# Cosine-similarity attention on one core: joint sums of squares as sixteen matmuls into one block of 64 columns, and new engine orders

## The chip, the core and the metric

The kernel runs on one core of one Trainium2 chip. The metric is the device time of one execution in microseconds (us). The profile shows one execution: PE is TensorE (matmuls), PEld its weight loads, DVE is VectorE, ACT is ScalarE, POOL is GpSimd, SP is the engine that issues most DMAs.

## What is computed

```python
Q_norm = Q / (np.linalg.norm(Q, axis=-1, keepdims=True) + 1e-10)
K_norm = K / (np.linalg.norm(K, axis=-1, keepdims=True) + 1e-10)
scores = np.einsum('bhqd,bhkd->bhqk', Q_norm, K_norm) / tau      # tau = 0.1
weights = np.exp(scores - np.max(scores, axis=-1, keepdims=True))
weights = weights / (np.sum(weights, axis=-1, keepdims=True) + 1e-10)
return np.einsum('bhqk,bhkd->bhqd', weights, V).astype(np.float32)
```

Q, K and V are float32 with 8 batches, 12 heads, 512 rows and 64 columns.

## The kernel before

The 96 heads are worked on in 48 pairs. Each pair s goes through the same steps, and the steps have keys that the order lists and this text use:

- LD and LV load Q, K and V of the pair (SP issues, 256 KB each) into rings of 15 and 10 buffers. VC casts V to bf16 beside a column of ones (POOL, L657).
- SQ squares Q and K of the pair into one bf16 tile `sq` of 16 groups (8 of Q, then 8 of K) of 64 values (POOL, L366).
- SSQ sums these squares in part on PE (L395): the identity is the weight operand, a slice of `sq` is the moving operand, and successive matmuls add up in PSUM, in columns of the bank `oops` that the products of the attention leave free. Part w = 0 is Q, w = 1 is K. For the 40 pairs in `SUM_BOTH` both parts go this way ("joint"); for a few others one part or none does.
- RED adds the rest of a row's partial sums on DVE (L404 for joint pairs, L408 for a single part, L412 without PE). NEW computes 1/sqrt of the sums in a few short DVE steps for a group of one to four pairs (L437, L441, L444).
- SCL scales Q and K to unit length (L479; Q on DVE, K on DVE or POOL), TR transposes them on PE (L488, four matmuls for Q and four for K), EVA copies the transposes out of PSUM (DVE, L506).
- SCO computes a 128-row chunk of the scores of both heads (PE, L625, two matmuls of 512 columns), EXP takes the exponential (ACT, L649). A pair has four chunks, the score tile has room for two, so the scores of a chunk need the exponential of two chunks before. For the last chunk of pairs 36 and 45 the exponential is a polynomial on DVE and POOL (SCX, X, Y) instead.
- PV multiplies with V (PE, L674): eight steps of four matmuls for each pair, into one bank of `oops` per head. RCP and NRM divide by the row sums on DVE (L690, L692), ST stores (SP, L696).

What stands when on which engine is written out by hand: `ORDER` lists for each of the five engines the numbers of the steps in the order in which they are issued. An engine takes its list from first to last. A step on PE or ACT waits for what it needs on other engines only; the order of its own list covers the rest.

Of the kernel before, what the change touches and what calls it, by code (L numbers as in the profile page):

```python
# [5 lines left out]
ALU = mybir.AluOpType  # L6
ACT = mybir.ActivationFunctionType
AX = mybir.AxisListType
# [100 lines left out]
def bass_cosine_similarity_attention_kernel(  # L109
# [23 lines left out]
    sq = [sb(f"sq{i}", [128, 16, DIM], bf16) for i in range(R_SQ)]  # L133
# [27 lines left out]
    P = Program(nc)  # L161
# [161 lines left out]
    def pair(s):  # L323
# [51 lines left out]
        for w in range(2):  # L375
# [12 lines left out]
            elif (s, w) in session:  # L388
                bank, due, before = session[s, w]

                at = 320 + (64 * w if both(s) else 0)

                def ssq(e, w=w, bank=bank, at=at):
                    for k in range(8):
                        last = e.matmul(  # L395
                            out=o_ps[bank][:, at : at + 64], lhsT=ident[:, :], rhs=sq[iqs][:, 8 * w : 8 * w + 8, 8 * k : 8 * k + 8],
                            start=(k == 0), stop=(k == 7))
                    return last

                P.add(("SSQ", s, w), "pe", "ssq", due, [*sqs, "eye"] + before, ssq)  # L400
                if both(s):
                    if w:
                        P.add(("RED", s, 1), "dve", "redj", due + 0.1, [*sums(s, 1), ("NRMS", 0, 0, 1), *new(g - R_X), *last_direct(s)],
                              lambda e, bank=bank, dst=x2[:, :, c8 : c8 + 8]: e.tensor_reduce(  # L404
                                  out=dst, in_=o_ps[bank][:, 320:448].rearrange("p (w g e) -> p w g e", w=2, e=8), axis=AX.X, op=ALU.add))
                    continue
# [379 lines left out]
def both(s):  # L786
    return s in SUM_BOTH
# [10 lines left out]
def slack(s, most):  # L798
# [23 lines left out]
    ),  # L822
    "dve": (
# [104 lines left out]
```

## Time and profile before

| | |
|---|---|
| three runs | 190.29, 355.23, 189.67 us (median 190.29) |
| the profiled execution | 189.59 us, its span from first to last instruction 187.7 us |
| granted TensorE clock | 0.999 of full speed |
| busy, of the span | PE 179.3 us, DVE 160.6 us, ACT 180.8 us, POOL 166.4 us |
| matmuls | 3009, of them 688 for sums of squares |

In the profile's rows a matmul's duration is its own, from start to end; matmuls that follow each other overlap, so the time that a burst takes is read from its start to the start of what follows. An exponential's duration overlaps the next one's in the same way. A row's bracket names the idle time of the engine before it and who ended it.

### The profile page before, as it was taken

The page shows a single profiled execution, that of the slowest core. Times are in us where ns is not written, and L with a number is a line of the kernel's source. Part 1 is how long each engine was busy: PE and PEld are TensorE (multiplying, and loading weights), DVE is VectorE, ACT ScalarE, POOL GpSimd, SP SyncE. Part 2 cuts the span into 40 slices and gives each one's busy share as a digit, 9 for nine tenths or more (in the row PEclk, how much of TensorE's full clock was granted, in tenths as well). Part 3 has the DMA queues.
Part 4 walks back from the last instruction along what each step waited for, and adds up shares of the span by engine and source line. Part 5 has one row for each costly group of instructions (what it writes and reads, how often), then busy time and mean ns, then how long its engine had stood idle before and what let it go on. Part 6 is the DMA issues. An engine that isn't in the chain of part 4 may idle for free.

```text
span 187.7 us, 7228 instructions
## 1 busy us (share of the span) xinstructions
PE 179.3 (96%) x3009; PEld 117.9 (63%) x3009; DVE 160.6 (86%) x523; ACT 180.8 (96%) x210; POOL 166.4 (89%) x147
## 2 busy tenths in 40 slices
PE   6989999999999999999999999999999999999983
PEld 2557666666666666666767766766566566555643
DVE  2699979897998779986887999999988999998744
ACT  5799999999999999999999999999999999999992
POOL 3799699999979999999989999999989999828950
PEclk9999999999999999999999999999999999999999
DMA  5999999899999958999999989998689923113315
GB/s 157 328 356 349 350 353 340 248 304 349 384 378 380 330 183 260 299 329 309 359 378 379 357 259 343 336 306 250 227 281 297 304 82 109 52 66 115 112 59 168
DMA packets 52447, 50.79 MB, mean 271 GB/s; under 512 B 3136, under 2 KB 52416, under 8 KB 52416
## 3 DMA queue, kind: packets, MB, share of 16 engines
q1 hardware_dynamic: 51984, 50.02, 81.3%
q8 instruction: 23, 0.38, 0.9%
q10 hardware_dynamic: 432, 0.33, 0.5%
q14 instruction: 8, 0.07, 0.1%
HBM read 37.75 MB, written 12.58 MB: 268 GB/s over the span
## 4 chain that ended last, share of the span: by engine, by line
ACT 83%; PE 10%; DVE 3%; POOL 2%; issue 1%; DVEq 0%; POOLq 0%
ACT et L649 83%; PE scps L625 3%; PE oops L674 2%; PE oops L195 2%; PE oops L395 1%; PE tps L488 1%; POOL sq L366 1%; DVE qt L294 1%; POOL qn L479 1%; DVE ob L692 0%; DVE qt L506 0%; DVE qn L479 0%; DVE ob L721 0%; POOL vb L657 0%; PE tps L283 0%
## 5 line engine op out<-in xcount | busy, mean ns | idle before, releaser
L649 ACT ACTIVATE et<-scps 128x1024 bf16<-128x1024 f32 (+1 forms) x191 | 174.5, 1056 | 0.5 <-PE scps L625 0.4
L366 POOL TENSOR_TENSOR sq<-qk 128x1024 bf16<-128x1024 f32 x44 | 82.8, 1893 | 0.4 <-DMA qk<-in_K_dram 0.3
L674 PE MATMUL oops<-vb,et 128*128 128x65 bf16 x1504 | 75.9, 194 | 0.6 <-DVE nps L437 0.2
L625 PE MATMUL scps<-qt 64*128 64x512 bf16 x380 | 74.4, 386 | 1.6 <-ACT et L649 1.0
L674 PEld LDWEIGHTS oops<-vb,et 128*128 128x128 bf16 x1504 | 57.0, 98 | 28.7 <-issue 19.8
L479 DVE TENSOR_TENSOR qn<-qk,nps 128x512 bf16<-128x512 f32 x67 | 44.1, 677 | 0.7 <-ACT nps L429 0.6
L692 DVE TENSOR_TENSOR ob<-oops,rd 128x256 f32<-128x256 f32 x94 | 39.3, 420 | 1.4 <-DVE ys L441 0.2
L506 DVE COPY qt<-tps 128x1024 bf16<-128x1024 bf16 x47 | 32.2, 685 | 4.3 <-PE tps L488 4.1
L488 PE MATMUL tps<-ident,qn 128*128 128x128 bf16 x376 | 34.3, 220 | 1.1 <-DVE qt L506 0.5
L657 POOL TENSOR_SCALAR vb<-vf 128x512 bf16<-128x512 f32 x48 | 29.2, 626 | 1.7 <-DVE qn L479 1.6
L395 PE MATMUL oops<-sq,ident 128*128 128x64 bf16 x688 | 30.0, 193 | 0.0
L479 POOL TENSOR_TENSOR qn<-qk,rk 128x512 bf16<-128x512 f32 x27 | 27.9, 1042 | 2.3 <-DVE rk L437 2.1
L395 PEld LDWEIGHTS oops<-sq,ident 128*128 128x128 bf16 x688 | 23.8, 98 | 7.5 <-issue 5.4
L625 PEld LDWEIGHTS scps<-qt 64*128 64x128 bf16 x380 | 18.3, 92 | 15.2 <-ACT et L649 3.4
L488 PEld LDWEIGHTS tps<-ident,qn 128*128 128x128 bf16 x376 | 21.7, 98 | 9.6 <-issue 4.8
L690 DVE RECIPROCAL rd<-oops 128x4 f32<-128x4 f32 x94 | 16.3, 176 | 7.8 <-PE oops L395 3.7
L404 DVE TENSOR_REDUCE nps<-oops 128x16 f32<-128x128 f32 x40 | 11.4, 286 | 4.2 <-PE oops L395 3.9
L437 DVE SCALAR_TENSOR_TENSOR nps<-nps,ys 128x32 f32<-128x32 f32 (+3 forms) x45 | 8.1, 193 | 0.5
L590 POOL TENSOR_TENSOR xw<-xz 128x1024 f32<-128x1024 f32 x2 | 3.8, 1892 | 4.9 <-DVE xz L569 4.9
L195 PE MATMUL oops<-warm_in,ident 128*128 128x512 bf16 x9 | 4.0, 631 | 1.7 <-POOL ident L185 1.7
L412 DVE TENSOR_REDUCE nps<-sq 128x8 f32<-128x512 bf16 x8 | 5.4, 684 | 0.0
L357 POOL TENSOR_TENSOR sq<-qk 128x512 bf16<-128x512 f32 (+1 forms) x5 | 4.6, 954 | 0.6 <-DMA qk<-in_K_dram 0.6
(62 smaller groups left out, 69.8 us busy)
## 6 DMA issues: line engine op xcount, KB each, us to landing
vf<-in_V_dram SPq DMA_DIRECT2D x48, 256.0 KB, 5.7
qk<-in_Q_dram SPq DMA_DIRECT2D x47, 256.0 KB, 4.7
qk<-in_K_dram SPq DMA_DIRECT2D x47, 256.0 KB, 5.7
out_dram<-ob SPq DMA_DIRECT2D x47, 256.0 KB, 4.1
qk<-in_Q_dram SPq DMA_DIRECT2D x2, 128.0 KB, 2.5
qk<-in_K_dram ACTq DMA_DIRECT2D x2, 128.0 KB, 2.7
out_dram<-ob SPq DMA_DIRECT2D x1, 128.0 KB, 2.0
out_dram<-ob SPq DMA_DIRECT2D x1, 64.0 KB, 1.8
```

What stands on the lines that cost most here:

```text
L366: lambda e: e.tensor_tensor(out=sqf, in0=data, in1=data, op=ALU.mult))
L395: last = e.matmul(out=o_ps[bank][:, at : at + 64], lhsT=ident[:, :], rhs=sq[iqs][:, 8 * w : 8 * w + 8, 8 * k : 8 * k + 8], start=(k == 0), ...
L404: lambda e, bank=bank, dst=x2[:, :, c8 : c8 + 8]: e.tensor_reduce(out=dst, in_=o_ps[bank][:, 320:448].rearrange("p (w g e) -> p w g e", w= ...
L479: lambda e, w=w, r=r: e.tensor_tensor(out=qn[iqn][:, w].rearrange("p t h d -> p h t d"), in0=qk[iq][:, w].rearrange("p h (t d) -> p h t d" ...
L488: last = e.transpose(t_ps[:, w, t, :], qn[iqn][:, w, t].rearrange("p h d -> p (h d)"), ident[:, :])
L506: lambda e, ws=ws: e.tensor_copy(out=qt[iqt][:, ws, :, :].rearrange("p w t x -> p (w t x)"), in_=t_ps[:, ws, :, :].rearrange("p w t x -> p ...
L625: last = e.matmul(out=sc_ps[:, 2 * b + h, :], lhsT=qt[iqt][64 * h : 64 * h + 64, 1, c, :], rhs=qt[iqt][64 * h : 64 * h + 64, 0, :, :], sta ...
L649: lambda e, c=c, b=b, hs=hs: e.activation(out=et[iet][:, c, hs[0] : hs[-1] + 1, :], in_=sc_ps[:, 2 * b + hs[0] : 2 * b + hs[-1] + 1, :], f ...
L657: return e.tensor_scalar(out=out, in0=in_, scalar1=1.0, scalar2=1.0, op0=ALU.mult, op1=ALU.mult)
L674: last = e.matmul(out=o_ps[h][:, 65 * t : 65 * t + 65], lhsT=et[iet][:, c, h, 128 * t : 128 * t + 128], rhs=vb[:, iq, c, h, :], start=(i = ...
L690: lambda e, hs=hs, grid=grid: e.reciprocal(out=rd[io][:, hs, :], in_=grid[:, :, :, DIM]))
L692: lambda e, hs=hs, grid=grid: e.tensor_tensor(out=ob[io][:, hs], in0=grid[:, :, :, 0:DIM], in1=rd[io][:, hs, :].unsqueeze(3).to_broadcast( ...
```

## The change

For joint pairs the sixteen matmuls now take all 16 groups at once and four columns of each, where each took 8 groups and eight columns. All sixteen add up into one block of 64 columns (320 to 384), where Q and K had one block of 64 columns each. Part w = 0 issues the first eight of the matmuls and part w = 1 the last eight, and part 1 comes after part 0. RED of a joint pair so adds four partial sums to each of 16 results, where it added eight.

```diff
-                at = 320 + (64 * w if both(s) else 0)
+                at = 320
 
                 def ssq(e, w=w, bank=bank, at=at):
+                    if both(s):
+                        for k in range(8 * w, 8 * w + 8):
+                            last = e.matmul(
+                                out=o_ps[bank][:, 320:384], lhsT=ident[:, :], rhs=sq[iqs][:, :, 4 * k : 4 * k + 4],
+                                start=(k == 0), stop=(k == 15), skip_group_check=True)
+                        return last
                     for k in range(8):
                         last = e.matmul(
                             out=o_ps[bank][:, at : at + 64], lhsT=ident[:, :], rhs=sq[iqs][:, 8 * w : 8 * w + 8, 8 * k : 8 * k + 8],
                             start=(k == 0), stop=(k == 7))
                     return last
 
-                P.add(("SSQ", s, w), "pe", "ssq", due, [*sqs, "eye"] + before, ssq)
+                P.add(("SSQ", s, w), "pe", "ssq", due, [*sqs, "eye"] + before + ([("SSQ", s, 0)] if both(s) and w else []), ssq)
                 if both(s):
                     if w:
                         ...
-                                  out=dst, in_=o_ps[bank][:, 320:448].rearrange("p (w g e) -> p w g e", w=2, e=8), axis=AX.X, op=ALU.add))
+                                  out=dst, in_=o_ps[bank][:, 320:384].rearrange("p (w g e) -> p w g e", w=2, e=4), axis=AX.X, op=ALU.add))
```

The lists of POOL, DVE and PE are written anew with the same steps in another order; those of ACT and SP stay. Two stretches of them, with the keys in place of the numbers:

```
POOL before: SQ 6, VC 2, VC 4, SQ 7, SCL 5 (K), VC 3, SQ 8, SCL 6 (K), SQ 9, VC 5, VC 6
POOL after:  SQ 6, VC 2, SQ 7, VC 4, VC 3, SCL 5 (K), SQ 8, SQ 9, SCL 6 (K), VC 5, SQ 10
PE before:   SCO (4,1), TR 5, TR 5, PV 3, SCO (4,2), PV 3 x4, SCO (4,3)
PE after:    SCO (4,1), PV 3 x3, SCO (4,2), TR 5, TR 5, PV 3, SCO (4,3)
```

Further on, POOL casts V of pair 16 right before V of pair 17 and behind the squares of pair 24, where it stood ahead of the squares of pair 19; V of pair 22 moves back in the same way.

124 rows, old and new, of the table ORDER are left out of this document.

## The prediction

> **What bounds the kernel now.** I read the page's busy shares first, then the shares of the chain of work that ended last, then that chain in order of time.
>
> ```profile
> span 187.7 us, 7228 instructions
> ...
> PE 179.3 (96%) x3009; PEld 117.9 (63%) x3009; DVE 160.6 (86%) x523; ACT 180.8 (96%) x210; POOL 166.4 (89%) x147
> ...
> ACT 83%; PE 10%; DVE 3%; POOL 2%; issue 1%; DVEq 0%; POOLq 0%
> ```
>
> ```profile
> 14.89 0.32 PE scps L625 x2
> 15.21 0.57 PE oops L395 x16
> ...
> 16.46 0.22 PE tps L488 x4
> 16.68 0.32 PE scps L625 x2
> 17.00 0.33 PE tps L488 x4
> ...
> 18.91 0.60 PE oops L674 x16
> ...
> 25.78 154.72 ACT et L649 x168
> ```
>
> From 25.78 us to 180.50 the chain is ACT alone: 168 exponentials in 154.72 us, 0.921 us each. How fast could they follow each other? The timeline of ACT shows a stretch in which none came late:
>
> ```profile
> 132.56 7.44 ACT L649 ACTIVATE et<-scps 128x1024 bf16<-128x1024 f32 x8
> ...
> 139.79 2.04 ACT L649 ACTIVATE et<-scps 128x1024 bf16<-128x1024 f32 x2
> ```
>
> Eight starts from 132.56 to 139.79 are 7.23 us, 0.904 us each. So in the long stretch (0.921 - 0.904) x 168 = 2.9 us are lost to scores that came late, and that is all that any ordering of the other engines can win there. The change leaves ACT's own list and instructions as they are.
>
> PE is nearly as full. One pair needs, by the chain's pieces, four score pairs at 0.32 us, two bursts of 16 products at 0.60, two sets of transposes at 0.22 and 0.33, and 16 sums at 0.57: 1.28 + 1.20 + 0.55 + 0.57 = 3.60 us. ACT needs 4 x 0.904 = 3.62 us for a pair. These pieces hold PE's changeovers between kinds of matmul. Without them the burst rows give the lower bound:
>
> ```profile
> 15.14 0.64 PE L395 MATMUL oops<-sq,ident 128*128 128x64 bf16 x16
> ...
> 25.67 0.66 PE L674 MATMUL oops<-vb,et 128*128 128x65 bf16 x16
> ```
>
> ```profile
> L674 PE MATMUL oops<-vb,et 128*128 128x65 bf16 x1504 | 75.9, 194 | 0.6 <-DVE nps L437 0.2
> L395 PE MATMUL oops<-sq,ident 128*128 128x64 bf16 x688 | 30.0, 193 | 0.0
> L404 DVE TENSOR_REDUCE nps<-oops 128x16 f32<-128x128 f32 x40 | 11.4, 286 | 4.2 <-PE oops L395 3.9
> L408 DVE TENSOR_REDUCE xs<-oops 128x8 f32<-128x64 f32 x4 | 0.9, 224 | 0.6 <-PE oops L395 0.6
> ```
>
> Sums follow each other every (640 - 193)/15 = 29.8 ns, products every (660 - 194)/15 = 31.1 ns. With these, 32 products take 0.99 us, 16 sums 0.48, the transposes 2 x 0.22, the scores 1.28: 3.19 us. PE's cover below ACT is so between 0.02 and 0.43 us for a pair.
>
> **The change part by part.**
>
> *The sums on PE.* Sixteen matmuls of 64 columns stay sixteen of 64 columns, with the same identity as weights. What differs is the moving operand: runs of four bf16 values (8 bytes) in 16 groups, where it was runs of eight (16 bytes) in 8 groups. No row of this trace has runs of four. The nearest: runs of eight cost 29.8/64 = 0.47 ns a column, the products' unbroken 65 columns 31.1/65 = 0.48, so cutting a row into 16-byte runs costs nothing. That is one end: 29.8 ns, and nothing below it, since the columns are as many. The other end takes the time as one per run: 29.8/8 = 3.7 ns a run, 16 runs, 59.6 ns. I take 29.8, by the rows where the cut was free. The upper end is 29.8 x 16 = 0.48 us more for each of 40 pairs; it is a rival below.
>
> The Trainium skill speaks here, on its page "SBUF — State Buffer", in "Specifications (TRN2)": lines of SBUF are 16 bytes, at least two hits on a line are needed for full speed, and each step to a new line pays a penalty. Each row of this trace makes eight new lines in 64 columns or so, so none tells the two halves of that rule apart. By the first half the new runs have four hits and stay free; by the second they cross sixteen lines instead of eight, and a matmul gets slower.
>
> *RED on DVE.* Its input goes from 128 columns to 64. The L408 row reads 64 columns in 224 ns and the L404 row reads 128 in 286; the new one has 64 columns in and 16 results, so between the two, nearer to 224. That saves up to 40 x 62 ns = 2.5 us of DVE. It isn't on the chain of the long stretch: ACT hides it. Bounds for the end are 0 and -2.5 us, the latter only if each late score came from DVE. The row's bracket says that RED itself mostly waits for PE (3.9 of 4.2 us), so I take 0 directly.
>
> *The order between the two parts.* SSQ 1 now needs SSQ 0; both are on PE, whose list holds them in that order, so nothing waits and nothing queues behind it.
>
> *POOL's list at the head of the long stretch.* The timeline there shows the largest single late start of the steady part:
>
> ```profile
> 20.99 0.62 POOL L657 TENSOR_SCALAR vb<-vf 128x512 bf16<-128x512 f32 x1 [1.57 <-DVE qn L479]
> 21.58 1.89 POOL L366 TENSOR_TENSOR sq<-qk 128x1024 bf16<-128x1024 f32 x1
> 23.43 1.04 POOL L479 TENSOR_TENSOR qn<-qk,rk 128x512 bf16<-128x512 f32 x1
> 24.44 0.63 POOL L657 TENSOR_SCALAR vb<-vf 128x512 bf16<-128x512 f32 x1
> ...
> ```
>
> ```profile
> 24.10 0.39 PE L625 MATMUL scps<-qt 64*128 64x512 bf16 x2
> ...
> 24.53 1.08 ACT L649 ACTIVATE et<-scps 128x1024 bf16<-128x1024 f32 x1
> ...
> 25.11 0.17 PEld L674 LDWEIGHTS oops<-vb,et 128*128 128x128 bf16 x4 [0.25 <-POOL vb L657]
> ...
> 25.78 1.02 ACT L649 ACTIVATE et<-scps 128x1024 bf16<-128x1024 f32 x1 [0.16 <-PE scps L625]
> ```
>
> POOL stood 1.57 us before the cast of V of pair 4 (by the code only its load can hold it; the named DVE step isn't among its needs), then squared pair 7, scaled K of pair 5, and cast V of pair 3 by 25.07. The products of pair 3 waited for that cast, the scores behind them came late, and ACT started at 25.78 where 24.53 + 0.904 = 25.43 was due: 0.35 us lost. After the change the squares of pair 7 stand ahead of that wait and the cast of pair 3 ahead of the scaling. SP issues the loads in order, at these times:
>
> ```profile
> 11.86 0.67 SPq L337 DMA_DIRECT2D qk<-in_K_dram  x1
> 12.57 1.37 SPq L340 DMA_DIRECT2D vf<-in_V_dram  x2
> ```
>
> K of pair 7 is 12.57 - 11.86 = 0.7 us ahead of V of pair 4, so it should be there by some 20.3 us (an estimate). From there 1.89 + 0.62 + 0.63 us give the cast of pair 3 at 23.4, and PE's new list wants it behind the scores that started at 24.10, at about 24.4. The wait goes, and with it 0.35 us (between 0 and 0.35). What is late next there is the scaling of K of pair 5, at 24.5 as before, for transposes that the new list puts one score pair later.
>
> *The rest of the lists.* With the costs above (0.32 for a score pair, 0.235 for eight sums, 0.23 for four transposes, 0.125 for four products) I counted how many of the 185 stretches from one score pair to the next hold more PE work than 0.904 us: 45 before, 37 after, together 1.8 and 1.5 us over. So PE's new list is no rougher. POOL's is tighter. In this window it has no pause at all:
>
> ```profile
> 69.20:83.70 14.50, 14.50 (x259) 9.76 (x257) 13.92 (x47) 14.50 (x17) 14.50 (x13) 1.00 0.85 272
> ...
> 112.60:127.10 14.50, 14.50 (x261) 9.94 (x258) 14.02 (x44) 14.50 (x17) 14.50 (x15) 1.00 0.99 324
> ```
>
> and the casts of V of pairs 16 and 22, which ran well ahead of their use, now come just before it:
>
> ```profile
> 56.93 1.21 POOL L657 TENSOR_SCALAR vb<-vf 128x512 bf16<-128x512 f32 x2
> ...
> 76.04 0.83 PE L674 MATMUL oops<-vb,et 128*128 128x65 bf16 x17
> ```
>
> The second of these two casts is pair 16's; it ended at 58.1, and its first product stands in the burst of 76.04. With the squares of pairs 18 to 24 now ahead of it, POOL's same work puts it near 75. Behind a product that waits, PE holds up the scores, and ACT waits for them; such a wait costs at most what pair 3's cost, 0.35. I put 0.2 us on the two (0 to 0.7). SP's list is unchanged, and the V buffers that these casts free are wanted by loads a whole ring of 10 pairs later, so no load moves onto the path (0).
>
> *Sum*, against the profiled execution's 189.59 us, 187.7 of span and 1.9 around it: 0 (sums) + 0 (RED) - 0.35 (pair 3's cast) + 0.2 (casts of 16 and 22) = 189.4. The median of the runs shown, 190.29, lies 0.7 us above that execution, and the other comparable run, 189.67, beside it.
>
> **The rivals.**
>
> *A: the short runs slow PE.* For it: no row shows runs of four; against it: runs of eight are as fast as unbroken rows. Place: the 16 sums of each of the 40 joint pairs. Price: at 59.6 ns, 0.48 us less the cover of 0.02 to 0.43, so 0.05 to 0.46 for a pair, 2 to 18 us; midway 10, giving 199.6 us, or 191.6 at the least. It decides from an extra of 0.02/16 = 1 ns to 0.43/16 = 27 ns a matmul. By the second half of the skill's rule this is the outcome, with a penalty that the page doesn't price.
>
> *B: POOL becomes what ends the waits.* For it: windows without a pause, and casts and squares moved to just before their use. Against it: POOL's work is the same, and 1.57 us of pause near 21 us can be filled. If eight of its steps come as late as pair 3's cast did, 8 x 0.35 = 2.8, less the 0.35 won: 192.0 us. Over 2% it would take eleven such.
>
> *C: the late starts vanish.* The 2.5 us from DVE and the smoother PE list let scores come in time throughout: 189.59 - 2.9 = 186.7 us. Against it: most late starts follow bursts on PE itself, whose work is not less.
>
> *D: RED gets no faster,* because sixteen results set its time rather than 128 columns: 286 ns again. Then only the lists act; the same 189.4, and the profile alone would show it.
>
> **How the numbers follow.** Forecast, with D in it (188.0 to 191.0): 0.74. B (191 to 193): 0.12. A: 0.09, of it 0.08 above 2%. C (186.7 to 188): 0.05. A measurement of this kernel tells about 2% from no change, 3.8 us. Faster by over that lies below even the floor of C: 0.02 for what I have not seen. Slower by over that: A's 0.08 and 0.02 of B: 0.10. The rest, 0.88, is within. The range leaves out A's upper part and C's lower: 187.4 to 192.8.
>
> **What would show it right or wrong.** The new RED rows at 220 to 240 ns; a burst of 16 sums still at 0.64 us; the cast of pair 3 near 23.4 us and no late exponential near 25.8; the chain still ACT for more than 80%, at 0.915 to 0.925 us an exponential. Bursts of sums over 0.75 us would mean A; products that wait for POOL's casts near 75 and 95 us, B. The forecast is wrong if exponentials follow each other slower than 0.935 us on average, or if the time leaves the range.

## The result, and the profile after

The changed kernel takes 189.17 us (median of 22 runs, 188.96 to 189.54), the kernel before 189.68 us (22 runs). The ratio is 0.9968, 95% interval 0.9956 to 0.9979: 0.3% faster, within the 2% that the forecast calls no change. The same kernel run again beside the experiments gave 189.24 against 189.55, ratio 0.9983 (0.9972 to 0.9993).

The page of the changed kernel and its chain in order of time (lines shifted by six, L649 is now L655):

```profile
span 186.9 us, 7229 instructions
...
PE 178.8 (96%) x3009; PEld 117.4 (63%) x3009; DVE 158.6 (85%) x523; ACT 180.5 (97%) x210; POOL 166.9 (89%) x147
...
ACT 92%; PE 3%; DVE 2%; DMA 1%; issue 0%; DVEq 0%
```

```profile
11.63 168.12 ACT et L655 x183
```

The chain is ACT for 92% of the span, where it was 83%: before, its first 17 us of exponentials ran through PE, POOL and DVE. The two shares are not a measure of time won, though. An exponential now takes 168.12/183 = 0.919 us where it took 0.921, and 0.904 is still the least that one takes from start to start.

```profile
L396 PE MATMUL oops<-sq,ident 128*128 128x64 bf16 x640 | 28.2, 192 | 0.0
L410 DVE TENSOR_REDUCE nps<-oops 128x16 f32<-128x64 f32 x40 | 8.8, 219 | 4.4 <-PE oops L396 4.2
```

The sums keep their duration (192 ns each, a burst of 16 in the timeline below 0.64 us as before), and RED went from 286 to 219 ns, 2.6 us less DVE work in all. DVE's busy time fell by 2.0 us and the kernel by 0.5.

Around the cast of V of pair 3 the timeline of POOL and PE reads now:

```profile
19.83 1.89 POOL L366 TENSOR_TENSOR sq<-qk 128x1024 bf16<-128x1024 f32 x1 [0.86 <-DMA qk<-in_K_dram]
21.69 1.21 POOL L663 TENSOR_SCALAR vb<-vf 128x512 bf16<-128x512 f32 x2
22.95 1.04 POOL L485 TENSOR_TENSOR qn<-qk,rk 128x512 bf16<-128x512 f32 x1
...
```

```profile
23.36 0.64 PE L396 MATMUL oops<-sq,ident 128*128 128x64 bf16 x16
...
24.25 0.54 PE L680 MATMUL oops<-vb,et 128*128 128x65 bf16 x12
```

Both casts of V (pairs 4 and 3, the row of two) are done by 22.9 us, and the first products of pair 3 start at 24.25 without a wait for POOL.

### The profile page after: what moved, and what is told of

The parts are those of the page before. It is cut to its first block, busy times and chain, and to the rows that moved or that the text cites. A ratio compares the mean times of both kernels' runs of the same rounds, so it can differ in the third digit from the quotient of the medians.

```text
span 186.9 us, 7229 instructions
## 1 busy us (share of the span) xinstructions
PE 178.8 (96%) x3009; PEld 117.4 (63%) x3009; DVE 158.6 (85%) x523; ACT 180.5 (97%) x210; POOL 166.9 (89%) x147
## 4 chain that ended last, share of the span: by engine, by line
ACT 92%; PE 3%; DVE 2%; DMA 1%; issue 0%; DVEq 0%
ACT et L655 91%; DMA qk<-in_Q_dram 1%; PE oops L680 1%; PE scps L631 1%; DVE xs L260 1%; DVE ob L727 0%; ACT ys L432 0%; ACT sq L254 0%; DVE ob L698 0%; PE tps L283 0%; ACT nps L435 0%; PE scps L283 0%; DVE qn L273 0%; PE oops L401 0%; PE oops L281 0%
## 5 line engine op out<-in xcount | busy, mean ns | idle before, releaser
L655 ACT ACTIVATE et<-scps 128x1024 bf16<-128x1024 f32 (+1 forms) x191 | 174.1, 1112 | 0.5 <-PE scps L631 0.5
L680 PE MATMUL oops<-vb,et 128*128 128x65 bf16 x1504 | 73.1, 194 | 0.0
L680 PEld LDWEIGHTS oops<-vb,et 128*128 128x128 bf16 x1504 | 55.7, 98 | 27.0 <-issue 19.0
L494 PE MATMUL tps<-ident,qn 128*128 128x128 bf16 x376 | 33.8, 220 | 0.5 <-DVE qn L485 0.5
L396 PE MATMUL oops<-sq,ident 128*128 128x64 bf16 x640 | 28.2, 192 | 0.0
L396 PEld LDWEIGHTS oops<-sq,ident 128*128 128x128 bf16 x640 | 22.5, 97 | 5.2 <-issue 4.3
L410 DVE TENSOR_REDUCE nps<-oops 128x16 f32<-128x64 f32 x40 | 8.8, 219 | 4.4 <-PE oops L396 4.2
L596 POOL TENSOR_TENSOR xw<-xw,xz 128x1024 f32<-128x1024 f32 x2 | 4.7, 2355 | 0.2
```

The costliest lines, as they stand in the source:

```text
L396: last = e.matmul(out=o_ps[bank][:, 320:384], lhsT=ident[:, :], rhs=sq[iqs][:, :, 4 * k : 4 * k + 4], start=(k == 0), stop=(k == 15), skip ...
L494: last = e.transpose(t_ps[:, w, t, :], qn[iqn][:, w, t].rearrange("p h d -> p (h d)"), ident[:, :])
L655: lambda e, c=c, b=b, hs=hs: e.activation(out=et[iet][:, c, hs[0] : hs[-1] + 1, :], in_=sc_ps[:, 2 * b + hs[0] : 2 * b + hs[-1] + 1, :], f ...
L680: last = e.matmul(out=o_ps[h][:, 65 * t : 65 * t + 65], lhsT=et[iet][:, c, h, 128 * t : 128 * t + 128], rhs=vb[:, iq, c, h, :], start=(i = ...
```

## The experiments

All ratios are against the kernel before, run beside the experiment on its chip; a ratio can differ by 0.1 to 0.2% from the quotient of the two medians. Two theories stood at the start: the gain comes from the new lists (theory lists), or from the shorter RED (theory shape). The prediction's own theory named one stretch of POOL's list.

### The new matmuls with the old lists

```diff
 ORDER: the lists of before; in PE's, SSQ (s, 0) and SSQ (s, 1) of a joint pair swapped where 1 stood first
```

> The new matmuls and the shorter RED with the lists of before (where the old PE list had part 1 of a joint pair ahead of part 0, the two swap places). Theory lists: the 0.5 us come from the new lists, so this stays at the kernel before, 189.4 to 189.9 us, with RED at 219 ns. Theory shape: 40 x 67 ns less DVE work is what lets scores come in time, so this gets 0.3 to 0.5 us of the gain, 189.2 to 189.4, and fewer late exponentials.

Measured: 189.27 us (11 runs) against 189.55 (35 runs), ratio 0.9999 (0.9981 to 1.0018). The interval doesn't tell a gain of 0.2 us from none; the profile tells more, below.

### The new lists with the old matmuls

```diff
 ORDER: the lists of after, with the matmuls and RED of before
```

> The new lists of POOL, DVE and PE with the old matmuls and the old RED of 286 ns. Theory lists: as fast as the changed kernel, 189.1 to 189.3 us. Theory shape: the new lists without the shorter RED give nothing or lose, 189.6 to 190.2.

Measured: 189.16 us (12 runs), ratio 0.9982 (0.9959 to 1.0005). That is the changed kernel's median, with an interval that just reaches 1.

### The head of POOL's list alone, and the stretch around pair 3 alone

```diff
-POOL: ones, eps, ones beside V, identity, SQ (0, K), ...
+POOL: eps, ones, identity, SQ (0, K), ones beside V, ...
```

> The kernel before with the first five steps of POOL's list alone in the new order (eps, ones, identity, squares of K of pair 0, ones beside V). Theory head: the identity is ready 0.3 us earlier, the warm-up matmuls start earlier, PE is at full clock when the first transposes come, and 0.2 us are won: 189.4 to 189.5 us, first exponential at 7.4 us. Rival: when PE's clock rises has nothing to do with 0.3 us, and the time stays at 189.7.

```diff
-POOL: ... VC 4, SQ 7, SCL 5 (K), VC 3, ...
+POOL: ... SQ 7, VC 4, VC 3, SCL 5 (K), ...
```

> The kernel before with one stretch of POOL's list alone in the new order: squares of pair 7, casts of V of pairs 4 and 3, K of pair 5. Theory of the prediction: the late exponential near 25.8 us goes and the time falls by 0.35 us, to 189.3. Rival: the wait goes, but later late starts grow by as much, since PE and POOL are nearly full: 189.6 to 189.8.

Measured: the head alone 189.56 us, ratio 0.9998 (0.9982 to 1.0014); the stretch alone 189.43 us, ratio 0.9999 (0.9986 to 1.0012). Neither is a gain that can be told from none, and the theory of the prediction, 0.35 us for the stretch, isn't borne out: the interval reaches down to 0.27 us less. The profile of the head alone gives a reason. Its POOL list still has the old stretch, and its cast of V of pair 3 ends at 25.08, as it did in the profile of before (25.07):

```profile
21.00 0.62 POOL L657 TENSOR_SCALAR vb<-vf 128x512 bf16<-128x512 f32 x1 [0.26 <-DMA vf<-in_V_dram]
...
24.45 0.63 POOL L657 TENSOR_SCALAR vb<-vf 128x512 bf16<-128x512 f32 x1
```

But there the exponential due next is not late:

```profile
24.36 2.01 ACT L649 ACTIVATE et<-scps 128x1024 bf16<-128x1024 f32 x2
...
25.28 2.00 ACT L649 ACTIVATE et<-scps 128x1024 bf16<-128x1024 f32 x2
```

One starts at 24.36, the next at 25.28, 0.92 us later (the rows overlap: the second exponential of the first row is the first of the second row). The one that was 0.35 late before now has until 26.2, and the products and scores ahead of it are through by then. In that execution ACT reached its long run 0.8 us later (12.61 us for the chain's first of 183) while POOL was held by the load of V until the same 21.00. The new matmuls with the old lists had the old stretch too: their exponentials came as early as the changed kernel's, but V of pair 4 was cast from 20.14 and V of pair 3 by 24.22, and nothing was late there either. So of three profiles with the old stretch only one has the loss, that in which the exponentials ran ahead of the loads. A profile is one execution, and this term of the sum was read from one that had the loss. How often the kernel before has it, one profile of it can't tell.

The chains of these profiles give the steady part, 183 exponentials from the fourth chunk of pair 0 on, apart from when it starts. In order: head alone, stretch alone, new matmuls alone, new lists alone, changed kernel again:

```profile
12.61 168.34 ACT et L649 x183
```

```profile
12.07 168.36 ACT et L649 x183
```

```profile
11.64 168.16 ACT et L655 x183
```

```profile
11.64 168.17 ACT et L649 x183
```

```profile
11.77 168.13 ACT et L655 x183
```

With old matmuls and, but for a few entries, old lists it takes 168.34 and 168.36 us; with either half of the change 168.16 and 168.17; with both 168.12 and 168.13. So each half alone takes 0.2 us off the late starts, and the two together hardly more. Whether they remove the same waits isn't shown. This is one execution of each, but the five fall in three groups that are 0.03 us wide or less, the last two 0.03 us apart.

The kernel before breaks its chain at the late exponential of pair 3, but its 183 can be counted in the same way from its timeline:

```profile
11.79 13.82 ACT L649 ACTIVATE et<-scps 128x1024 bf16<-128x1024 f32 x15
```

The chains above start 0.07 us behind the row of their first exponential (11.63 against 11.56 in the changed kernel). So its 183 run from 11.86 to 180.50, 168.64 us: 0.30 more than with the head alone, which is about what that execution lost at pair 3, and 0.52 more than the changed kernel.

### POOL's list alone, the lists of PE and DVE alone

```diff
 ORDER: POOL's list of after, all else of before
```

> The kernel before with POOL's new list alone. Theory POOL: its list holds the gain of the new lists (0.5 us in median span), so 189.1 to 189.3 us. Rival PE: POOL's list alone is tuned for another order of PE and gives nothing or loses, 189.5 to 190.5.

```diff
 ORDER: PE's and DVE's lists of after, POOL's and the matmuls of before
```

> The kernel before with the new lists of PE and DVE alone, POOL's as before. Theory PE: the smoother PE list (37 overfull stretches in place of 45) holds the gain, 189.1 to 189.3 us. Rival POOL: without the casts moved to it, 189.5 to 190.5.

Measured: POOL's list alone 196.32 us (4 runs), ratio 1.0361 (1.0337 to 1.0384); the other two alone 199.79 us (6 runs), ratio 1.0521 (1.0484 to 1.0558). Both theories fall: neither part holds the gain, and each part alone costs 7 and 10 us. The lists of waits of the two kernels say what happens:

```profile
POOL qn L479 <- DVE rk L437: 6.1, 5, 2.6
ACT et L649 <- PE scps L625: 6.0, 7, 2.2
```

```profile
POOL qn L479 <- DVE rk L437: 10.5, 6, 4.5
ACT et L649 <- PE scps L625: 9.1, 11, 3.3
...
PEld oops L395 <- POOL sq L366: 7.0, 9, 2.6
```

(total us, times, longest.) POOL stands before the scaling of a K whose norm DVE's other list delivers later, PE stands before sums whose squares POOL's other list delivers later, and ACT waits 6 and 9 us for scores. What each list gives is worth nothing by itself.

A part of this loss is the clock's. Here is the longest wait of PE in the second kernel, and the row of its page with the granted clock in tenths, in 40 slices of 4.95 us:

```profile
79.75 1.03 PE L395 MATMUL oops<-sq,ident 128*128 128x64 bf16 x16 [2.53 <-POOL sq L366]
80.72 0.61 PE L625 MATMUL scps<-qt 64*128 64x512 bf16 x2
```

```profile
PEclk9999999999999999586999999999999999999999
```

PE stood for 2.53 us, and behind it the granted clock was 0.50 from 80 to 86 us: sixteen sums took 1.03 us and two scores 0.61, where 0.64 and 0.39 are usual. The same came behind a wait of 1.67 us that ended at 88.69, but not behind one of 1.64 us that ended at 77.98 in the first kernel; what decides it isn't shown. Of ACT's 9.1 us of waits 2.5 lie in these two stretches, and of the first kernel's 6.0 about 1.0 lie in one near 126 us, behind a wait of PE of 2.08 us. Most of the loss is thus the waits themselves, and the clock adds to it.

### The warm-up without the identity

```diff
-last = e.matmul(out=o_ps[1], lhsT=ident[:, :], rhs=warm_in[:, :], ...)   # 9 times
+last = e.matmul(out=o_ps[1], lhsT=warm_in[:, 0:128], rhs=warm_in[:, :], ...)   # 10 times
```

> The changed kernel with ten warm-up matmuls that take the zeros as weights too, so they need not wait for the identity. Theory head: PE's clock rises earlier, in all runs before the first transposes near 5.6 us, and the first exponentials no longer start late: 0.1 to 0.3 us faster than the changed kernel, 188.9 to 189.1, and less scatter. Rival: the head is set by the first loads and the DVE steps behind them, and nothing changes.

Measured: 189.22 us (12 runs) beside the changed kernel's 189.24 (11 runs) on the same chip, ratio to the kernel before 0.9992 (0.9975 to 1.0009). The rival holds: nothing changes that can be measured. In this profile four of the first transposes take 0.41 us at 5.70, as in the changed kernel's (0.64 before), but they wait for DVE:

```profile
5.70 0.41 PE L283 MATMUL tps<-ident,qn 128*64 128x128 bf16 x4 [0.53 <-DVE qn L273]
```

No other kernel here was faster than the changed one by more than the scatter.

### How short a run of the moving operand may be

```diff
-rhs=sq[iqs][:, :, 4 * k : 4 * k + 4]
+rhs=sq[iqs][:, :, :].rearrange("p g (a k c) -> p g a k c", a=2, c=2)[:, :, :, k, :]
```

> The changed kernel with other columns in each joint matmul: from each of the 16 groups two runs of two values (4 bytes) instead of one run of four. The same sixteen matmuls of 64 columns. Theory free runs: the time of a matmul goes by its columns, so a burst of 16 stays at 0.64 us and the kernel at 189.2. Rival A of the prediction: the time goes by runs; then runs of two cost more even if runs of four did not, a burst of 16 takes over 0.75 us and the kernel 2 us or more.

```diff
+rhs=sq[iqs][:, :, k : 64 : 16]
```

> The changed kernel with four single values, 16 apart, from each of the 16 groups in each joint matmul: every column is a run of its own. Theory free runs: still 0.64 us for 16 and 189.2 us. Rival A: 64 runs a matmul, so the burst takes 1.1 us or more (twice 29.8 ns a matmul) and the kernel 191.6 to 207.

Measured: runs of two 205.06 us, ratio 1.0822 (1.0719 to 1.0926); runs of one 247.69 us, ratio 1.3072 (1.2953 to 1.3191), two runs of each. PE's timeline, runs of two and then runs of one:

```profile
24.56 1.07 PE L396 MATMUL oops<-sq,ident 128*128 128x64 bf16 x16
25.56 0.39 PE L631 MATMUL scps<-qt 64*128 64x512 bf16 x2
```

```profile
22.72 1.10 PE L396 MATMUL oops<-sq,ident 128*128 128x64 bf16 x8
23.76 0.39 PE L631 MATMUL scps<-qt 64*128 64x512 bf16 x2
```

The groups of both give the mean duration of one, 232 and 296 ns:

```profile
L396 PE MATMUL oops<-sq,ident 128*128 128x64 bf16 x640 | 45.4, 232 | 0.0
```

```profile
L396 PE MATMUL oops<-sq,ident 128*128 128x64 bf16 x640 | 84.3, 296 | 0.0
```

So one follows the other every (1070 - 232)/15 = 56 ns with runs of two, and every (1100 - 296)/7 = 115 ns with runs of one. Runs of four and of eight take 29.9 and 29.8. So rival A's mechanism is real, and the change stops right ahead of it: 32 and 64 runs a matmul cost 1.75 and 1.8 ns each, and 16 runs at that price would be 28 to 29 ns (an estimate), about what 64 columns take anyway. The Trainium skill's page "SBUF — State Buffer", "Specifications (TRN2)", asks for two hits on a 16-byte line for full speed. Runs of two have two hits on a line and take twice the time: here two hits were not enough, and four were. Every run of these kernels lies in a line of its own, so whether the price is for a run or for a line, they don't tell.

### PE's cover, by more work on PE

```diff
+for k in range(0 if w else 8):        # and 16 in the second kernel
+    e.matmul(out=o_ps[bank][:, 384:448], lhsT=ident[:, :], rhs=sq[iqs][:, :, 4 * (k % 16) : 4 * (k % 16) + 4], ...)
 for k in range(8 * w, 8 * w + 8):
```

> The changed kernel with 8 more matmuls of 64 columns ahead of each joint pair's sums, into columns that nothing reads: 0.24 us more PE work for each of 40 pairs. It measures PE's cover below ACT, which the prediction put between 0.02 and 0.43 us a pair. At 0.02 the kernel gets 40 x 0.22 = 8.8 us slower, 198; at 0.43 it stays at 189.2. From rows in which scores already come 0.04 to 0.3 us ahead of their exponential I expect 3 to 6 us: 192 to 195.

> The same with 16 more matmuls: 0.48 us more PE work a pair, the full price that rival A would have had. At a cover of 0.02 us 40 x 0.46 = 18.4 us slower, 207.6; at 0.43 us 2 us slower, 191.2. With both kernels the cover follows from the difference: once PE binds, 8 more matmuls must cost 40 x 0.24 = 9.5 us.

Measured: 8 more 198.77 us (two runs, 197.78 and 199.76), ratio 1.049 (1.0246 to 1.0735); 16 more 206.70 us (two runs), ratio 1.0909 (1.0809 to 1.1008). The page of the second: PE is the chain.

```profile
PE 78%; ACT 15%; DVE 4%; DMA 1%; issue 1%; POOL 0%; DVEq 0%
```

Sixteen matmuls at 29.8 ns are 0.477 us, 19.1 us for 40 pairs; 206.7 - 189.2 = 17.5 came out at the end. The cover is (19.1 - 17.5)/40 = 0.04 us a pair. The two runs with 8 more lie 2 us apart. The profiled one, 199.76, reached its long run of exponentials only at 14.00 us, where the kernel with 16 more had it at 11.46; the other, 197.78, cost 8.5 us for 9.5 of work, a cover of 0.02. Runs of two agree: a burst of 16 takes 25.56 - 24.56 = 1.00 us up to the next scores, and the changed kernel's 0.57, so 40 x 0.43 = 17.2 us more PE work cost 15.8. My own expectation of 3 to 6 us for 8 more matmuls was wrong. Scores that come 0.04 to 0.3 us ahead of their exponential are not spare time that adds up: a score can't start before the exponential two chunks back has ended, so its lead says nothing of how much PE could still take on. The sum over a pair's pieces did.

## Why the prediction was right, point by point

*What bounds the kernel.* Right: ACT's exponentials at 0.904 us with some 2.7 us of late starts (183 x 0.015), and PE beside it. Of the two bounds for PE's cover, 0.02 by the chain's pieces and 0.43 by bursts alone, the first is the true one (0.02 to 0.04). The changeovers between kinds of matmul belong to the work.

*The sums on PE: 0.* Right, at 29.9 ns. But the upper end, a price for each run, was no far-fetched one: runs of two showed it at once. Only the price was too high, 3.7 ns a run where 1.75 to 1.8 were measured.

*RED: 0 directly, 219 ns in place of 286.* The duration is right but for a nanosecond (forecast 220 to 240). At the end it was not nothing: with the new matmuls and the old lists the steady part is 0.2 us shorter. On top of the new lists it is worth next to nothing (0.04).

*Pair 3's cast: -0.35.* This is the step that was mis-sized. The wait went as forecast (cast done at 22.9, forecast 23.4; K of pair 7 was there at 19.8, not 20.3), and in the profiled execution it had cost about what was read off (0.30 of the steady part). But alone its removal bought nothing that could be measured, and the two other profiles with the old stretch don't have the loss.

*Casts of pairs 16 and 22: +0.2.* Mis-sized the other way. In the changed kernel the cast of pair 16 is the first of the three in this row, done by 73.5, and its first products stand in the burst behind it, from 74.07 on, which waits for no cast:

```profile
72.88 1.80 POOL L663 TENSOR_SCALAR vb<-vf 128x512 bf16<-128x512 f32 x3
```

```profile
73.94 0.66 PE L680 MATMUL oops<-vb,et 128*128 128x65 bf16 x16
```

Pair 22 is the same: its cast, the first of a row of two at 94.08, ends at 94.70, and its first products start at 95.30. Both casts come 0.6 us ahead of their use.

*The sum.* 189.4 from 189.6, a fall of 0.2; measured -0.5 and, when run again, -0.3. The total is near, of terms that were not: the loss that I removed was not typical, the one that I added did not come, and the shorter RED, which I put at nothing, took 0.2 off the steady part when it came without the new lists. That the sum came within 0.3 us is luck; that the time would move by far less than 2% is not, as it follows from ACT's bound and the 29.9 ns.

*Rivals.* A did not happen with runs of four, did with runs of two, and once PE was loaded cost what was worked out (15.8 us, range 2 to 18). B, POOL's list as what ends the waits, is what comes out when the lists don't fit together (196.3), but not with all three. C's floor of 186.7 wasn't neared. D is refuted by the 219 ns.

*What stays open.* The steady part gives 0.2 of the 0.3 to 0.5 us. What comes behind it takes 7.1 to 7.2 us in all these profiles, so the rest lies in losses like that at pair 3 or in when the long run of exponentials starts, 11.63 to 11.77 us in the profiles of the changed kernel and the new lists, 12.07 and 12.61 in those of the old lists with one stretch new. But new matmuls with the old lists began at 11.64 too, and the kernel before itself started this chunk's exponential at 11.79 where the changed one did at 11.56, so this moves from execution to execution (in the chain of the changed kernel it is a first load, of Q, that sets it). That the new lists let an early start through which the old ones can lose again at pair 3 would fit these numbers; it is argued, not shown, and the new matmuls with the old lists began early and lost nothing there.

## What to carry to other kernels

Where two engines are both full, work out the need of each for one turn of the loop with the changeovers in it, and test the cover by adding work; the leads in the timeline are not spare time. A late start that one profile shows may belong to that execution: before a term rests on it, look for it in a second one. Orders written out by hand for several engines belong together: half of a new set can cost ten or more times what the whole set gains.

## What the runs showed of the hardware

How finely a matmul's moving operand is cut costs nothing down to runs of four bf16 values (29.9 ns for 64 columns) and then goes by the runs, 1.75 to 1.8 ns each: 56 ns for runs of two, 115 for runs of one. A one-line change of the slice, with as many instructions, so moves this kernel from 189 to 248 us.

The price of a run doesn't go by TensorE's granted clock. With runs of one the clock was 0.50 from 94 to 106 us, with PE busy throughout, and a burst of eight sums took the same 1.10 us as at full clock (22.72 above), while sixteen products took 1.06 us in place of 0.66:

```profile
101.19 1.10 PE L396 MATMUL oops<-sq,ident 128*128 128x64 bf16 x8
...
104.93 1.06 PE L680 MATMUL oops<-vb,et 128*128 128x65 bf16 x16
```

So some of the way to 248 us is this stretch of slower products and scores; why the clock fell, the trace doesn't show.
